# Blocks of up products as seven products of sums, in the second feed-forward network of a diffusion step

## The chip, the cores and the metric

The kernel runs on one core of one Trainium2 chip. The time is that of one execution on the device, in microseconds (us). TensorE (PE, with its weight loads as PEld) multiplies, VectorE (DVE) and ScalarE (ACT) do element-wise work, GpSimd (POOL) has next to none here, and SyncE (SP) issues the transfers from memory (DMA). Each engine takes its own instructions in order; between engines they wait on semaphores.

## The reference

One inference step of a two-layer backbone, for 128 context tokens and 512 latent tokens of 1024 features. Layer 0 mixes tokens by a state-space scan, layer 1 by differential attention; a gated convolutional feed-forward network follows in each layer. That network is what the change touches:

```python
def conv_ffn(h, up_w, conv_w, conv_b, down_w):
    u = dwconv(h @ up_w, conv_w, conv_b)
    a, v = jnp.split(u, 2, axis=-1)
    return (jax.nn.silu(a) * v) @ down_w
```

`up_w` is 1024 x 5632 (2 x 2816), `down_w` 2816 x 1024; `dwconv` is a convolution over tokens of width 3, for each channel apart. All is in 32-bit floating point.

## The kernel before, in words

Activations stand with features on the 128 partitions and all 640 tokens (512 latent, then 128 context) along the columns: `h` is 8 tiles of 128 x 640, one for each feature tile k. To keep the accuracy of 32 bits with products of lower precision, every operand is split into a high part (`hi`, a rounded copy made by ScalarE) and a low part (`lo`, the difference, made by VectorE), and each product of tiles is three: high with high, high with low, low with high.

Weights come in units of at most 128 x 1024. `weight_units` (L1214) lists them in the order of their use. `prefetch` (L119) issues the transfer of a unit into one of four `raw` buffers (`RAW`), on the queue of SP; `cast` (L128) makes `whi` (ScalarE, L95) and `wlo` (VectorE, L101), in one of five pairs of buffers (three with tag `w`, two with tag `x`). `nextw` (L147) hands out the next unit, prefetches three ahead and casts one ahead.

`ffn` (L601) works in three stages (`SUB`): up products for 9, 7 and 6 pairs of tiles, each stage followed by the down products of the part that is done. A pair p is one tile of the gate half a and one of the value half v of the hidden features. `dense_many` (L158) makes one up tile `up` of 128 x 640 in a PSUM buffer of two banks (1024 columns, three buffers with tag `d`): for each of 8 feature tiles three products, each in two column parts of 256 and 384 columns ("A", "B"), 48 products in all. The first three up tiles of a network are made ahead in `start_tiles` (L316; named `st`), while the normalisation still delivers `h` half by half; so pair 0 and half of pair 1 come from there.

After each tile `copy_out` (L607) copies it to `uraw` (ScalarE). `epilogue` (L613) then does for both halves the convolution (`conv`, L593: one ScalarE scaling, then four VectorE steps, of 511 and 127 columns twice), a Silu on ScalarE (`ca`), the gate product on VectorE (`cv`), and the split of the result into `mh` and `ml`, which the down products (`po`) take. `gate_add` (L278) adds the down tiles to the residual `xr` on VectorE.

The framework lays out each engine's instructions ahead of time, from the order in which the program emits them, their dependencies and priorities; what it has laid out is a fixed queue for each engine when the program runs. Dependencies are followed tile by tile: a write to one part of a PSUM tile waits for a reader of the other part.

Of the kernel before, what the change touches and what calls it, by code (L numbers as in the profile page):

```python
# [18 lines left out]
P = 128  # L19
D = 1024  # L20
KT = D // P
TP = 128
TS = 512
T = TP + TS
# [11 lines left out]
FT = FH // P  # L36
SUB = ((0, 8), (8, 15), (15, 22))
DA_SCALE = 64 ** -0.5
LAM_INIT = 0.8 - 0.6 * math.exp(-0.3 * 1)
RAW = 4  # L40
ATT_SPLIT = 6
NF = 19
RSQRT_MAGIC = float(0x5F3759DF)
# [2 lines left out]
class Step:  # L46
# [53 lines left out]
    def tt(self, out, a, b, op):  # L100
        return self.nc.vector.tensor_tensor(out, a, b, op)  # L101

    def mm(self, out, lhsT, rhs, start, stop):
        return self.nc.tensor.matmul(out, lhsT, rhs, start=start, stop=stop)  # L104

    def ct(self, shape, name, dt=F32):
        return self.pc.tile(shape, dt, tag=name, name=name)
# [11 lines left out]
    def prefetch(self, upto):  # L119
        while len(self.wraw) <= min(upto, len(self.units) - 1):  # L120
            u = len(self.wraw)
            ap, n = self.units[u]
            r = self.pw.tile([P, 1024], F32, tag="raw", name=f"raw{u}", bufs=RAW)
            dst = r[:, :n]
            self.nc.sync.dma_start(dst.rearrange("p (i c) -> p i c", i=ap.shape[1]) if len(ap.shape) == 3 else dst, ap)
            self.wraw[u] = r

    def cast(self, upto):  # L128
        while len(self.wcast) <= min(upto, len(self.units) - 1):
            u = len(self.wcast)  # L130
            self.prefetch(u)
            n = self.units[u][1]
            r = self.wraw[u]
            wp, t, b = (self.pw, "w", 3) if self.px is None or u % 5 < 3 else (self.px, "x", 2)
            hi = wp.tile([P, 1024], F32R, tag=t + "hi", name=f"whi{u}", bufs=b)
            lo = wp.tile([P, 1024], F32R, tag=t + "lo", name=f"wlo{u}", bufs=b) if u else None
            if u == 0:
                half = lambda t, j: t.rearrange("p (k j m) -> p k j m", k=KT, j=2)[:, :, j, :]
                r3 = r[:, :n].rearrange("p (k m) -> p k m", k=KT)
                self.act(half(hi, 0), r3, AF.Copy)  # L140
                self.tt(half(hi, 1), r3, half(hi, 0).bitcast(F32), ALU.subtract)
            else:
                self.act(hi[:, :n], r[:, :n], AF.Copy)
                self.tt(lo[:, :n], r[:, :n], hi[:, :n].bitcast(F32), ALU.subtract)
            self.wcast[u] = (hi, lo)

    def nextw(self):  # L147
# [411 lines left out]
    def mod_rest(self, l, t0, pool):  # L559
# [5 lines left out]
        for c in range(2):  # L565
            sb = self.pw.tile([P, 1024], F32, tag="raw", name="csil", bufs=RAW)
            self.act(sb, cb[:, c, :], AF.Tanh, scale=0.5)
# [33 lines left out]
    def ffn(self, l, h, nextnorm, pool):  # L601
        nc = self.nc
        cw = pool.tile([P, 2 * FT, 4], F32, tag="fcw", name=f"fcw{l}", bufs=1)
        nc.sync.dma_start(cw, self.a["fcw"][l])
        mid = {}

        def copy_out(ps):  # L607

            u = self.slot("f", "uraw", bufs=NF)
            self.act(u, ps[:, PO:PO + T], AF.Copy)  # L610
            return u

        def epilogue(p, ua, uv):  # L613
            ca = self.tmp("ca")
            self.conv(ca, ua, cw[:, p, :])
            cv = self.tmp("cv")
            self.conv(cv, uv, cw[:, FT + p, :])
            self.act(ca, ca, AF.Silu)
            self.tt(cv, ca, cv, ALU.mult)
            hi = self.slot("mh", f"mh{p}", F32R, bufs=9, pool=pool)  # L620
            lo = self.slot("ml", f"ml{p}", F32R, bufs=9, pool=pool)
            self.act(hi, cv, AF.Copy)
            self.tt(lo, cv, hi.bitcast(F32), ALU.subtract)
            mid[p] = (hi, lo)

        def pair(p):
            ua = copy_out(self.next_tile(h, "up"))
            epilogue(p, ua, copy_out(self.next_tile(h, "up")))

        self.start_tiles(h)  # L630
        done = 0
        for s, (k0, k1) in enumerate(SUB):
            self.down = False
            while done < min(k1 + 1, FT):
                pair(done)
                done += 1
            self.down = True
            if s == len(SUB) - 1 and self.modtask:
# [530 lines left out]
    def attention(self, h, nextnorm, pool):  # L1169
# [8 lines left out]
        for hd in range(8):  # L1178
# [35 lines left out]
    def weight_units(self):  # L1214
        a = self.a
        u = [(a["w_dt"], 512)]
        xbc = lambda g: [16 + 4 * g + t for t in range(4)] + [32 + g, 36 + g]
        z = lambda g: [4 * g + t for t in range(4)]
        order = xbc(0) + xbc(1) + z(0) + xbc(2) + z(1) + xbc(3) + z(2) + z(3)
        u += [(a["w_in"][j], 1024) for j in order]  # L1220
        for hf in range(2):
            u += [(a["w_so"][i, :, hf * 1024:(hf + 1) * 1024], 1024) for i in range(KT)]

        def ffn(l):
            done = 0
            out = []
            for k0, k1 in SUB:
                while done < min(k1 + 1, FT):
                    out.extend([(a["w_up"][l, done], 1024), (a["w_up"][l, FT + done], 1024)])
                    done += 1  # L1230
                out.extend([(a["w_dn"][l, i, :, k0 * P:k1 * P], (k1 - k0) * P) for i in range(KT)])
            return out

        u += ffn(0)
        for hd in range(8):
            u += [(a["w_qkv"][8 * j + hd], 1024) for j in range(3)]
        c = ATT_SPLIT * P
# [143 lines left out]
```

## Time and profile before

| | |
|---|---|
| median of 3 runs | 1879.16 us (1878.75 to 1879.62) |
| profiled execution | 1880.65 us |
| its span | 1878.9 us |
| TensorE busy | 1838.2 us, 98% of the span |
| VectorE busy | 1369.5 us, 73% |
| ScalarE busy | 952.9 us, 51% |
| chain that ended last | PE 91%, DVE 4%, ACT 3%, DMA 1% |

The page gives the busy time of each engine, the chain of work that ended last (followed back from the last instruction, each step to what released it), and groups of instructions by line, engine, operation and tiles: busy time and the mean duration of one in ns, then the idle time of the engine just before them and what ended it. Most operations go through helpers, so a line number says only which helper it was (L104 a product, L95 ScalarE, L98 and L101 VectorE), and the tile names tell what it was for. In lines in order of time, the first number is the start in us from the start of the span, the second the length; equal neighbours are merged (`x4`). Views of a stretch give busy time of PE, PEld, DVE, ACT and POOL, then the granted TensorE clock as a share of full speed.

### The profile page before, as it was taken

How to read it: one execution, taken by the hardware profiler on the slowest of the kernel's cores; microseconds unless marked ns; L12 is line 12 of the kernel's file. 1: busy time of each engine (PE TensorE's matmuls, PEld its weight loads, DVE VectorE, ACT ScalarE, POOL GpSimd, SP SyncE). 2: the span in 40 equal slices, each digit the busy share in tenths (PEclk: the TensorE clock that was granted, in tenths of full speed). 3: DMA queues.
4: the chain of work that ended last, by engine and by line, in shares of the span. 5: the costliest groups of instructions: out<-in, count | busy, mean ns of one | idle time of the engine just before them, and what ended most of it. 6: DMA issues, size and time to landing. Idle time of an engine off the chain costs nothing.

```text
span 1878.9 us, 32832 instructions
## 1 busy us (share of the span) xinstructions
PE 1838.2 (98%) x13322; PEld 1741.9 (93%) x13322; DVE 1369.5 (73%) x2637; ACT 952.9 (51%) x1745; POOL 0.2 (0%) x4
## 2 busy tenths in 40 slices
PE   7999999999999999999999999999999999999997
PEld 5899999999999999999999988888899999999996
DVE  5699999999658999974555877788777543553554
ACT  3489687878336441441443656566445432431441
POOL 0000000000000000000000000000000000000000
PEclk9999999999999999999999999999999999999998
DMA  9835243436624556532222212111122222122211
GB/s 337 266 121 147 97 147 109 140 115 202 199 80 142 185 180 221 181 103 91 68 68 78 79 40 65 58 50 48 61 88 89 69 79 80 63 72 89 64 40 57
DMA packets 79679, 209.74 MB, mean 112 GB/s; under 512 B 9276, under 2 KB 16040, under 8 KB 79400
## 3 DMA queue, kind: packets, MB, share of 16 engines
q1 hardware_dynamic: 78952, 207.13, 33.5%
q8 instruction: 104, 1.70, 0.4%
q10 hardware_dynamic: 576, 0.52, 0.1%
q14 instruction: 47, 0.39, 0.1%
HBM read 201.66 MB, written 5.96 MB: 111 GB/s over the span
## 4 chain that ended last, share of the span: by engine, by line
PE 91%; DVE 4%; ACT 3%; DMA 1%; issue 1%; SPq 0%; DVEq 0%; ACTq 0%
PE up L104 31%; PE po L104 25%; PE z L104 6%; PE x L104 5%; PE st L104 5%; PE bc L104 3%; PE yp L104 3%; PE q L104 2%; PE v L104 2%; PE k L104 1%; PE modrow L104 1%; PE sl L104 1%; PE in L104 1%; ACT whi L95 1%; ACT e L95 1%; PE ov L104 1%
## 5 line engine op out<-in xcount | busy, mean ns | idle before, releaser
L95 ACT ACTIVATE whi<-raw 128x1024 fp32r<-128x1024 f32 (+3 forms) x227 | 234.2, 1033 | 387.2 <-PE po L104 239.6
L101 DVE TENSOR_TENSOR wlo<-raw,whi 128x1024 fp32r<-128x1024 f32 (+2 forms) x226 | 269.2, 1192 | 172.2 <-ACT whi L95 165.1
L98 DVE SCALAR_TENSOR_TENSOR xr<-po,mod,xr 128x256 f32<-128x256 f32 (+2 forms) x231 | 89.2, 433 | 162.0 <-PE po L104 161.8
L104 PE MATMUL po<-mh,whi 128*128 128x256 f32 (+1 forms) x704 | 167.8, 310 | 0.0
L104 PE MATMUL po<-ml,whi 128*128 128x256 f32 (+1 forms) x704 | 167.5, 310 | 0.0
L104 PE MATMUL po<-mh,wlo 128*128 128x256 f32 (+1 forms) x704 | 167.3, 310 | 0.0
L104 PE MATMUL up<-h11h,wlo 128*128 128x256 f32 (+1 forms) x656 | 149.4, 309 | 0.0
L104 PE MATMUL up<-h01h,wlo 128*128 128x256 f32 (+1 forms) x656 | 149.4, 308 | 0.0
L104 PE MATMUL up<-h01h,whi 128*128 128x256 f32 (+1 forms) x656 | 149.3, 308 | 0.0
L104 PE MATMUL up<-h01l,whi 128*128 128x256 f32 (+1 forms) x656 | 149.3, 308 | 0.0
L104 PE MATMUL up<-h11l,whi 128*128 128x256 f32 (+1 forms) x656 | 149.3, 308 | 0.0
L104 PE MATMUL up<-h11h,whi 128*128 128x256 f32 (+1 forms) x656 | 149.3, 308 | 0.0
L104 PEld LDWEIGHTS po<-mh,whi 128*128 128x128 f32 x704 | 128.5, 188 | 0.7 <-ACT mh L95 0.5
L104 PEld LDWEIGHTS po<-mh,wlo 128*128 128x128 f32 x704 | 128.8, 188 | 0.0
L104 PEld LDWEIGHTS po<-ml,whi 128*128 128x128 f32 x704 | 128.6, 188 | 0.0
L104 PEld LDWEIGHTS up<-h01h,whi 128*128 128x128 f32 x656 | 119.3, 188 | 0.0
L104 PEld LDWEIGHTS up<-h01h,wlo 128*128 128x128 f32 x656 | 119.3, 188 | 0.0
L104 PEld LDWEIGHTS up<-h01l,whi 128*128 128x128 f32 x656 | 119.3, 188 | 0.0
L104 PEld LDWEIGHTS up<-h11h,whi 128*128 128x128 f32 x656 | 119.2, 188 | 0.0
L104 PEld LDWEIGHTS up<-h11h,wlo 128*128 128x128 f32 x656 | 119.2, 188 | 0.1
L104 PEld LDWEIGHTS up<-h11l,whi 128*128 128x128 f32 x656 | 119.2, 188 | 0.0
L98 DVE SCALAR_TENSOR_TENSOR ca<-uraw,fcw,ca 128x511 f32<-128x511 f32 (+1 forms) x176 | 85.2, 546 | 11.6 <-ACT ca L95 11.6
(497 smaller groups left out, 4315.6 us busy)
## 6 DMA issues: line engine op xcount, KB each, us to landing
raw<-in_w_up SPq DMA_DIRECT2D x88, 512.0 KB, 3.5
mw<-in_modT SPq DMA_DIRECT2D x48, 512.0 KB, 3.5
raw<-in_w_in SPq DMA_DIRECT2D x40, 512.0 KB, 5.5
rb<-rowd SPq DMA_DIRECT2D x40, 512.0 KB, 5.6
raw<-in_w_dn SPq DMA_DIRECT2D x32, 448.0 KB, 3.2
raw<-in_w_qkv SPq DMA_DIRECT2D x24, 512.0 KB, 3.5
mr<-in_mod SPq DMA_DIRECT2D x44, 256.0 KB, 5.7
mp<-in_modp SPq DMA_DIRECT2D x32, 256.0 KB, 5.4
```

What stands on the lines that cost most here:

```text
L95: return self.nc.scalar.activation(out, in_, func, **k)
L98: return self.nc.vector.scalar_tensor_tensor(out, in0, s, in1, op0, op1)
L101: return self.nc.vector.tensor_tensor(out, a, b, op)
L104: return self.nc.tensor.matmul(out, lhsT, rhs, start=start, stop=stop)
```

## The change

From pair 2 on (`S0`), in the second network alone, a pair of up tiles is computed together by `pair7`. Its four first feature tiles (k = 0 to 3) are taken as a product of 2 x 2 blocks: the weights have two blocks of two feature tiles in each half (a and v), the activations have two blocks of feature tiles and two blocks of 320 tokens (`TH`). Such a product needs eight products of blocks; here it is made of seven (`block`, each 2 feature tiles x 3 terms), on sums and differences of blocks, with some results used in more than one of the four output blocks. Feature tiles 4 to 7 (`rest`) are multiplied as before, but in column halves of 320.

On the side of the activations the sums (`t12`, `t43`) and their high and low parts (`Th`, `Tl`, `T3`) are made once, by `operands`, when pair 2 begins. On the side of the weights they are made for each pair by a unit without a transfer (`ap is None`), which stands in the list between the unit of a and that of v: four VectorE sums of 256 columns, then two casts of 512 on ScalarE and two on VectorE. The v unit's cast leaves out its first 256 columns. On the output side one accumulator is copied out while it grows (`ua` left, then `ua` right with `p5` added, then `uv`), and others are added from PSUM on VectorE. `epilogue` is as before. `prefetch` runs six units ahead in `pair7`.

```diff
@@ cast
+            elif sums:
+                self.prefetch(u + 1)
+                ra, rv = self.wraw[u - 1], self.wraw[u + 1]
+                w = NS * P
+                s12, s34 = (self.slot("f", nm, bufs=NF) for nm in ("s12", "s34"))
+                self.tt(s12[:, :w], rv[:, :w], rv[:, w:2 * w], ALU.add)
+                self.tt(s12[:, w:2 * w], s12[:, :w], ra[:, :w], ALU.subtract)
+                self.tt(s34[:, :w], ra[:, :w], rv[:, :w], ALU.subtract)
+                self.tt(s34[:, w:2 * w], ra[:, w:2 * w], s12[:, w:2 * w], ALU.subtract)
+                for j, s in enumerate((s12, s34)):
+                    c = slice(2 * w * j, 2 * w * (j + 1))
+                    self.act(hi[:, c], s[:, :2 * w], AF.Copy)
+                    self.tt(lo[:, c], s[:, :2 * w], hi[:, c].bitcast(F32), ALU.subtract)
             else:
-                self.act(hi[:, :n], r[:, :n], AF.Copy)
-                self.tt(lo[:, :n], r[:, :n], hi[:, :n].bitcast(F32), ALU.subtract)
+                c = slice(c0 // 2, n)
+                self.act(hi[:, c], r[:, c], AF.Copy)
+                self.tt(lo[:, c], r[:, c], hi[:, c].bitcast(F32), ALU.subtract)
...
@@ ffn
+        def block(ps, w, c0, xs, first, last, more=False):
+            hi, lo = w
+            for i, (xh, xl) in enumerate(xs):
+                c = slice(c0 + i * P, c0 + (i + 1) * P)
+                self.mm(ps, hi[:, c], xh, first and i == 0, False, more)
+                self.mm(ps, hi[:, c], xl, False, False, more)
+                self.mm(ps, lo[:, c], xh, False, last and i == len(xs) - 1, more)
+                if i % 2:
+                    self.hook()
+
+        def operands():
+            cut = lambda t, j: t[:, j * TH:(j + 1) * TH]
...
+            for i in range(NS):
+                f1, f2 = self.tmp("f1"), self.tmp("f2")
+                for f, k in ((f1, i), (f2, NS + i)):
+                    self.tt(f, h[k][0].bitcast(F32), h[k][1].bitcast(F32), ALU.add)
+                t12, t43 = self.slot("f", "t12", bufs=NF), self.slot("f", "t43", bufs=NF)
+                self.tt(cut(t12, 0), cut(f1, 1), cut(f1, 0), ALU.subtract)
+                self.tt(cut(t12, 1), cut(f2, 1), cut(t12, 0), ALU.subtract)
+                self.tt(cut(t43, 0), cut(f2, 0), cut(t12, 1), ALU.subtract)
+                self.tt(cut(t43, 1), cut(f2, 1), cut(f1, 1), ALU.subtract)
...
+                for o, x in ((slice(0, T), t12), (slice(T, T + TH), cut(t43, 0))):
+                    self.act(hi[:, o], x, AF.Copy)
+                    self.tt(lo[:, o], x, hi[:, o].bitcast(F32), ALU.subtract)
+                self.act(cut(t3, 0), cut(t43, 1), AF.Copy)
+                self.tt(cut(t3, 1), cut(t43, 1), cut(t3, 0).bitcast(F32), ALU.subtract)
...
+        def pair7(p, B, Ts, rest):
...
+            self.prefetch(u + 6)
+            self.cast(u + 2)
...
+            ps = self.dense_ps("up")
+            X, Y = ps[:, :TH], ps[:, 512:512 + TH]
+            block(X, wa, 0, B11, True, True)
+            with self.tc.high_priority():
+                self.act(ua[:, lft], X, AF.Copy)
+            block(Y, wa, w, B21, True, False)
+            ps = self.dense_ps("up")
+            V, Z = ps[:, :TH], ps[:, 512:512 + TH]
+            block(V, ws, 0, T1, True, True)
+            with self.tc.high_priority():
+                self.act(p5, V, AF.Copy)
+            block(X, ws, w, T2, False, True, True)
+            with self.tc.high_priority():
+                self.tt(ua[:, rgt], X, p5, ALU.add)
+            block(Y, wa, r0, rest[0], False, True)
+            self.tt(ua[:, lft], Y, ua[:, lft], ALU.add)
+            block(Z, ws, 3 * w, B22, True, False)
+            self.cast(u + 3)
+            block(Z, wa, r0, rest[1], False, True)
+            self.tt(ua[:, rgt], Z, ua[:, rgt], ALU.add)
+            block(X, ws, 2 * w, T3, False, True, True)
+            with self.tc.high_priority():
+                self.act(uv[:, rgt], X, AF.Copy)
+            self.cast(u + 4)
+            block(V, wv, r0, rest[1], False, True, True)
+            self.tt(uv[:, rgt], V, uv[:, rgt], ALU.add)
+            block(X, wv, w, T4, False, True, True)
+            block(X, wv, r0, rest[0], False, True, True)
+            self.act(uv[:, lft], X, AF.Copy)
+            epilogue(p, ua, uv)
+
         def pair(p):
+            if l and p >= S0:
+                if p == S0:
+                    self.sevens = operands()
+                return pair7(p, *self.sevens)
...
@@ weight_units
-                    out.extend([(a["w_up"][l, done], 1024), (a["w_up"][l, FT + done], 1024)])
+                    sums = [(None, 1024)] if l and done >= S0 else []
+                    out.extend([(a["w_up"][l, done], 1024), *sums, (a["w_up"][l, FT + done], 1024)])
```

More of the change, by code (lines that the diff above doesn't have):

```diff
@@ L40 @@
 RAW = 4
+NS = 2
+S0 = 2
+TH = T // 2
 ATT_SPLIT = 6
@@ L101, in tt, with mm @@
         return self.nc.vector.tensor_tensor(out, a, b, op)
-    def mm(self, out, lhsT, rhs, start, stop):
-        return self.nc.tensor.matmul(out, lhsT, rhs, start=start, stop=stop)
+    def mm(self, out, lhsT, rhs, start, stop, more=False):
+        return self.nc.tensor.matmul(out, lhsT, rhs, start=start, stop=stop, skip_group_check=more)
     def ct(self, shape, name, dt=F32):
@@ L122, in prefetch @@
             ap, n = self.units[u]
+            if ap is None:
+                self.wraw[u] = None
+                continue
             r = self.pw.tile([P, 1024], F32, tag="raw", name=f"raw{u}", bufs=RAW)
@@ L133, in cast @@
             r = self.wraw[u]
+            sums = self.units[u][0] is None
+            c0 = 2 * NS * P if u and self.units[u - 1][0] is None else 0
             wp, t, b = (self.pw, "w", 3) if self.px is None or u % 5 < 3 else (self.px, "x", 2)
@@ L624, in epilogue @@
             mid[p] = (hi, lo)
+        def block(ps, w, c0, xs, first, last, more=False):
[9 more added lines that the diff above has]
+            cut = lambda t, j: t[:, j * TH:(j + 1) * TH]
+            B = [[[tuple(cut(t, j) for t in h[NS * k + i]) for i in range(NS)] for j in range(2)] for k in range(2)]
+            Ts = [[], [], [], []]
+            for i in range(NS):
[7 more added lines that the diff above has]
+                self.tt(cut(t43, 1), cut(f2, 1), cut(f1, 1), ALU.subtract)
+                hi, lo = (pool.tile([P, 3 * TH], F32R, tag=f"T{nm}{i}", name=f"T{nm}{i}", bufs=1) for nm in "hl")
+                t3 = self.slot("f", f"T3_{i}", F32R, bufs=NF)
+                for o, x in ((slice(0, T), t12), (slice(T, T + TH), cut(t43, 0))):
[3 more added lines that the diff above has]
+                self.tt(cut(t3, 1), cut(t43, 1), cut(t3, 0).bitcast(F32), ALU.subtract)
+                Ts[0].append((cut(hi, 0), cut(lo, 0)))
+                Ts[1].append((cut(hi, 1), cut(lo, 1)))
+                Ts[2].append((cut(t3, 0), cut(t3, 1)))
+                Ts[3].append((cut(hi, 2), cut(lo, 2)))
+            rest = [[tuple(cut(t, j) for t in h[k]) for k in range(2 * NS, KT)] for j in range(2)]
+            return B, Ts, rest
@@ new lines, in pair7 @@
+        def pair7(p, B, Ts, rest):
+            (B11, _), (B21, B22) = B
+            T1, T2, T3, T4 = Ts
+            u = self.wi
+            self.wi += 3
+            self.prefetch(u + 6)
+            self.cast(u + 2)
+            wa, ws, wv = (self.wcast[u + j] for j in range(3))
+            w, r0 = NS * P, 2 * NS * P
+            ua, uv = (self.slot("f", "uraw", bufs=NF) for _ in range(2))
+            p5 = self.slot("f", "p5", bufs=NF)[:, :TH]
+            lft, rgt = slice(0, TH), slice(TH, T)
+            ps = self.dense_ps("up")
[28 more added lines that the diff above has]
+            epilogue(p, ua, uv)
```

## The prediction

> **What bounds the kernel now.** I read the page's busy shares first, then the chain of work that ended last, then busy time by stretch, then the groups by shape inside the second feed-forward network, and last the order of time on VectorE and ScalarE where the change begins.
>
> ```profile
> PE 1838.2 (98%) x13322; PEld 1741.9 (93%) x13322; DVE 1369.5 (73%) x2637; ACT 952.9 (51%) x1745; POOL 0.2 (0%) x4
> ...
> 1416.16 105.73 PE up L104 x720
> 1521.90 56.00 PE po L104 x384
> 1577.90 98.64 PE up L104 x672
> ...
> 1726.47 84.53 PE up L104 x576
> ...
> 1430.00:1521.00 91.00, 91.00 (x623) 91.00 (x622) 52.08 (x79) 43.73 (x53) 0.00 (x0) 1.00 0.25 82
> ```
>
> The first line is the page's engine table, the next four are steps of the chain (start, length, what), the last is busy time in one stretch (sum, then PE, PEld, DVE, ACT, POOL, granted clock, DMA share, GB/s). In the second network TensorE works without a gap: the three runs of up products last 105.73, 98.64 and 84.53 us, and in 91 us of the first TensorE is busy for 91, VectorE for 52, ScalarE for 44. The full clock is granted. So TensorE products alone set the time there, and fewer of them would shorten it, as long as the other two engines keep up.
>
> ```profile
> L104 PE MATMUL up<-h11l,whi 128*128 128x384 f32 x328 | 110.8, 338 | 0.0
> L104 PE MATMUL up<-h11h,wlo 128*128 128x256 f32 x328 | 91.6, 279 | 0.0
> ...
> L98 DVE SCALAR_TENSOR_TENSOR ca<-uraw,fcw,ca 128x511 f32<-128x511 f32 x44 | 32.9, 748 | 7.7 <-ACT ca L95 7.7
> L98 DVE SCALAR_TENSOR_TENSOR xr<-po,mod,xr 128x256 f32<-128x256 f32 x42 | 18.4, 480 | 75.8 <-PE po L104 75.8
> L101 DVE TENSOR_TENSOR cv<-ca,cv 128x640 f32<-128x640 f32 x22 | 18.1, 825 | 0.7
> L98 DVE SCALAR_TENSOR_TENSOR ca<-uraw,fcw,ca 128x127 f32<-128x127 f32 x44 | 15.2, 345 | 0.0
> L98 DVE SCALAR_TENSOR_TENSOR h11l<-nt,mod,h11h 128x256 fp32r<-128x256 f32 x8 | 3.8, 481 | 0.0
> L101 DVE TENSOR_TENSOR nsq<-nsq,sqt 128x256 f32<-128x256 f32 x4 | 1.7, 416 | 0.0
> ...
> L95 ACT ACTIVATE uraw<-up 128x640 f32<-128x640 f32 x41 | 28.2, 687 | 0.0
> L95 ACT ACTIVATE mh<-cv 128x640 fp32r<-128x640 f32 x22 | 16.2, 738 | 57.3 <-DVE cv L101 57.3
> L95 ACT ACTIVATE sqt<-xr 128x384 f32<-128x384 f32 x4 | 2.1, 527 | 0.9 <-DVE xr L98 0.9
> ```
>
> These are groups by shape from 1400 us on (busy, mean ns of one, idle before). A duration is not a price: products overlap. 105.73 / 720 gives 0.1468 us from one product to the next, at a mean of 320 columns; the records of a 384 and a 256 together last 617 ns but take 294, so a result stands about 0.2 us behind the end of its columns (estimate). For VectorE and ScalarE the price comes from the starts of neighbours in order of time:
>
> ```profile
> 1420.95 1.22 DVE L101 TENSOR_TENSOR wlo<-raw,whi 128x1024 fp32r<-128x1024 f32 x1
> 1422.09 0.82 DVE L101 TENSOR_TENSOR cv<-ca,cv 128x640 f32<-128x640 f32 x1
> 1422.82 1.67 DVE L98 SCALAR_TENSOR_TENSOR ca<-uraw,fcw,ca 128x511 f32<-128x511 f32 x3
> ...
> 1425.14 0.34 DVE L98 SCALAR_TENSOR_TENSOR ca<-uraw,fcw,ca 128x127 f32<-128x127 f32 x1
> 1425.41 1.22 DVE L101 TENSOR_TENSOR wlo<-raw,whi 128x1024 fp32r<-128x1024 f32 x1
> 1426.54 1.93 DVE L98 SCALAR_TENSOR_TENSOR cv<-uraw,fcw,cv 128x511 f32<-128x511 f32 x4
> 1428.39 1.22 DVE L101 TENSOR_TENSOR wlo<-raw,whi 128x1024 fp32r<-128x1024 f32 x1
> ...
> 1443.34 0.82 DVE L101 TENSOR_TENSOR ml<-cv,mh 128x640 fp32r<-128x640 f32 x1 [0.81 <-ACT mh L95]
> ...
> 1423.92 0.68 ACT L95 ACTIVATE uraw<-up 128x640 f32<-128x640 f32 x1
> 1424.50 1.05 ACT L95 ACTIVATE whi<-raw 128x1024 fp32r<-128x1024 f32 x1
> 1425.46 0.91 ACT L95 ACTIVATE cv<-uraw,fcw 128x640 f32<-128x640 f32 x1
> 1426.27 0.72 ACT L95 ACTIVATE ca<-ca 128x640 f32<-128x640 f32 x1
> ```
>
> Start to start a tensor-tensor operation of 1024 columns holds VectorE for 1.13 us (1425.41 to 1426.54), one of 640 for 0.73 (1422.09 to 1422.82), the four convolution steps for 1.85, the step of 127 for 0.27. A straight line through 640 and 1024 gives estimates of 0.39 for 320, 0.32 for 256, 0.59 for 512 and 0.87 for 768 columns. ScalarE: 0.58 for a copy of 640, 0.96 for 1024, 0.81 for a scaled 640.
>
> **Part 1: products saved.** A pair of up tiles is 96 products before (2 tiles, 8 feature tiles, 3 terms, 2 column parts) and 90 after: seven blocks of 6, and four of 12 for the feature tiles left as they are. All 90 have 320 columns, the mean of before, and load weights as often as before, once each. 20 pairs (2 to 21) take part: 120 x 0.1468 = 17.6 us, a pair 13.21 instead of 14.09. This is the ceiling, and all of it is on the path.
>
> **Part 2: the operands, once.** The sums of feature blocks are emitted at pair 2, and VectorE takes its queue in order. The third product of pair 2's third block waits for the low part of the first half of the weight sums; in the changed program's order this stands behind everything that follows. Up to the step at 1425.14 the queue is that of before, less 0.27 for a cast of 768 columns in place of 1024 at 1420.95, so this step starts at 1424.87. From it on: that step 0.27; four f of 640 columns, 2.92; one convolution 1.85; the gate product and ml of pair 1, 1.46; eight differences of 320, 3.12; Tl, two of 640 and two of 320, 2.24; the low parts of T3, two of 320, 0.78; a cast of 1024 for pair 3, 1.13; four weight sums of 256, 1.28. Together 15.05, to 1439.9. ScalarE's high part of 512 columns (about 0.63, between 527 and 738 ns) starts when the third weight sum is done, 0.3 earlier, and VectorE's low part needs about 0.69 more (between 416 and 825 ns): TensorE goes on at 1441.0. ScalarE is done with each of its shares before VectorE wants it, so its queue adds nothing else.
>
> TensorE would want that product at 1416.16 + 48 x 0.1468 (the fourth tile) + 14 x 0.1468 = 1425.2. It stands for about 15.8 us. What is queued behind on TensorE is all of pair 2, and nothing else is there to fill in: after the first block the second waits too, for a ScalarE copy that stands behind the T copies, so that the gap is some 14 us in one piece. Bounds: 14.5 us if each of the 30 operations holds the queue 0.04 less; 18.5 if each costs its full duration, 0.09 more (825 against 730 ns).
>
> **Part 3: the clock after it.**
>
> ```profile
> 1082.20:1085.60 3.40, 1.15 (x12) 0.88 (x12) 3.02 (x5) 1.71 (x6) 0.00 (x0) 1.00 0.27 77
> 1085.60:1089.00 3.40, 3.22 (x12) 3.22 (x13) 1.21 (x3) 2.21 (x6) 0.00 (x0) 0.50 0.22 82
> ```
>
> In attention TensorE was busy for 1.15 of 3.4 us, and in the next 3.4 us half the clock was granted, with 12 products done. At half clock 3.4 us of work take 1.7 us too long. A gap of 14 us earns at least that. I take 1.7, with 0 and 3.4 (two such stretches) as ends. [...]
>
> **Part 4: what a pair costs after that.** VectorE per pair before: 3.70 for two convolutions, 1.46, two casts 2.26: 7.4 of 14.1. After: 3.70, 1.46, casts of 1024, 768 and twice 512 (3.18), four sums of 256 (1.28), four adds of 320 out of PSUM (1.56): 11.2 of 13.2. In order, it also waits twice on ScalarE, 0.8 for the high part of the weight sums (after the last ua add ScalarE scales 0.81, copies about 0.35, casts 1024 in 0.96 and 512 in 0.63, to 3.3 with the first hand-over, when VectorE has three sums and one convolution step behind it, 2.5) and 0.81 for mh, as in the row of 1443.34: about 13.1. It fits, by 0.1 to 0.4 us. No row has a 320-column add out of PSUM. The xr row (PSUM, 480 ns) and the h11l row (SBUF, 481) at 256 columns say that PSUM costs nothing more, so 0.39; ends 0.32 (256 columns) and 0.73 (640). [...]
>
> ScalarE: copies of 320 four times (about 0.3 each), 3.0 for casts, 1.6 for convolutions, 1.3 for silu and mh: 7.1 of 13.2. Room enough, but one of its copies is on the path. The accumulator of the first block is copied to ua before TensorE may write the next block into the same tile. In the steady order ScalarE has, from the end E of the pair before: the last uv copy (from E + 0.2, about 0.45 long, between the halved 687 ns and 527), the convolution scaling (from E + 0.65, holds 0.81), and only then the ua copy, from E + 1.46 to E + 1.9. TensorE has 11 products in between, 1.61. It waits 0.3 us in each pair. Ends: 0 if ScalarE takes the copy first, 0.8 if the copies last as long as those of 640. The other exchanges have room: the p5 add 13 products, the T3 copy 12, the ua adds 6 (0.88 against about 0.7, the tightest).
>
> So a pair takes 13.5, with 13.2 and 14.8 as ends; 14.8 is VectorE at full durations with no overlap: 2.99 + 1.38 + 1.65 + 3.56 (casts) + 1.66 + 1.92, and the two waits of 0.8. I take 13.5, nearest to the starts of neighbours, which is how back-to-back work of this queue ran. Sixteen pairs save 0.57 each, and pairs 2, 3, 9 and 16, where VectorE has no pair behind it or has caught up, up to 0.88: 9.1 + 3.0 to 3.5, taken as 12, or 11 with the tight ua adds slipping now and then.
>
> ```profile
> raw<-in_w_up SPq DMA_DIRECT2D x88, 512.0 KB, 3.5
> ```
>
> **At no cost.** The row is the page's group of up weight loads (count, size, us from issue to landing). The weight sums move no byte: the queue of loads has the same entries in the same order, two of 512 KB a pair, and each raw buffer is given back one pair ahead; without that lead 3.5 us of a load would show. At the two returns from the down products the weight sums of the next pair are cast before the last down tile, with VectorE idle there; without this each return would pay 1.28 + 0.63 + 0.69 us, less the 1.76 of two blocks. The final epilogue has the length of before.
>
> **The sum.** + 15.8 + 1.7 - 11 = + 6.5 us. The profiled execution took 1880.65 us (span 1878.9, 1.75 around it), the median of the runs is 1879.16, 0.08% below; the difference carries over: about 1886 us.
>
> **Rivals.**
> 1. The per-pair wait is hidden (ScalarE's copy comes in time, and the ua adds too). For it: ScalarE is half idle; against: its order is fixed, with the convolution first. Saving 17.6: 1879.16 + 17.5 - 17.6 = 1879, no change.
> 2. VectorE becomes the bound. For it: 13.1 of 13.2, with no row for its new shapes. From 14.1 a pair nothing is saved: 1879.16 + 17.5, 1896; at the end of 14.8, 1911.
> 3. Faster: TensorE's stop at pair 2 is short. It decides from 13.8 us all told with the full saving (17.6 - 13.8 = 3.8, 0.2%); at 10 us it would be 1872. For it: the feature tiles are ready before the first up tile starts, so the work has no data to wait for. Against: it needs VectorE to run 15 us of queued work in 10, and the queue keeps its order.
> 4. The count does not turn into time, because 320 columns run slower than the mean of 256 and 384. Before has no full-height row of it; both ends are linear, so I give this little: at 0.160 a product a pair is 14.4, and the time 1879 + 17.5 + 6, 1903.
>
> **Chances.** A measurement of this kernel tells about 0.2% (3.8 us) from no change: below 1875.4 is faster, above 1882.9 slower. Forecast (13.4 to 13.8 a pair, 1882 to 1892): 0.58. Rival 1: 0.17. Rival 2: 0.16. Rival 3: 0.06. Rival 4: 0.03. Rival 1 lies within 0.2% but for 0.01 below it, and 0.03 of the forecast lies within too. So faster 0.07, same 0.19, slower 0.74. The range goes from rival 1 to the near side of rival 2, 1879 to 1895 (left out are rivals 3 and 4 and some 0.1 of rival 2); the likeliest case alone has 1882 to 1892.
>
> **What would show it.** A TensorE gap of about 14 us after the first block of pair 2, with VectorE busy on f, t, Tl and s throughout, and half the clock once behind it; up products 120 fewer at 0.147 us each; then a short TensorE wait on the ScalarE uraw copy in nearly every pair; pairs 13.5 us apart. It is wrong if the gap is under 10 us, if pairs are over 13.9 apart with TensorE waiting for VectorE's adds, or if the products themselves take longer.

## The result and the profile after

The changed kernel takes 1885.07 us (median of 10 runs, 1881.10 to 1888.89), the kernel before, run beside it, 1878.89 us (10 runs, 1877.45 to 1881.52). The ratio is 1.0032, with a 95% interval of 1.0023 to 1.0042: slower by about 6 us. The profiled execution took 1887.62 us with a span of 1885.8, against 1880.65 and 1878.9 before: 6.9 us more in the span.

First the engine table of the changed kernel's page, its largest group of up products, and what TensorE waited for from 1400 us on (us in total, times, longest):

```profile
PE 1829.6 (97%) x13202; PEld 1727.3 (92%) x13202; DVE 1455.7 (77%) x2855; ACT 973.0 (52%) x1831; POOL 0.2 (0%) x4
...
L107 PE MATMUL up<-h11h,whi 128*128 128x320 f32 (+1 forms) x456 | 141.2, 316 | 14.9 <-ACT uraw L98 14.6
...
PE up L107 <- ACT uraw L98: 14.6, 6, 13.7
PE nbc L107 <- DVE rs_y L101: 2.5, 1, 2.5
PE ms L107 <- ACT sq L98: 0.7, 1, 0.7
PE up L107 <- ACT whi L98: 0.4, 1, 0.4
```

There are 120 products fewer, and TensorE is busy for 8.6 us less than the 1838.2 of before. In their place stands 14.6 us of waiting for ScalarE's copies of up products, 13.7 of it in one piece. That piece in the order of time, on TensorE and then on VectorE (start, length, what, and in brackets the idle time before it and its releaser):

```profile
1437.12 0.64 PE L107 MATMUL up<-h11h,whi 128*128 128x320 f32 x1 [13.65 <-ACT uraw L98]
1439.50 0.64 PE L107 MATMUL up<-Th,whi 128*128 128x320 f32 x1 [0.41 <-ACT whi L98]
1440.23 0.64 PE L107 MATMUL up<-Th,wlo 128*128 128x320 f32 x1
```

```profile
1423.73 0.35 DVE L101 SCALAR_TENSOR_TENSOR ca<-uraw,fcw,ca 128x127 f32<-128x127 f32 x1
...
1428.44 0.50 DVE L104 TENSOR_TENSOR t<-f,f 128x320 f32<-128x320 f32 x1
1428.85 0.50 DVE L104 TENSOR_TENSOR t<-f,t 128x320 f32<-128x320 f32 x1
...
1439.48 1.29 DVE L104 TENSOR_TENSOR wlo<-s,whi 128x512 fp32r<-128x512 f32 x2 [0.24 <-ACT whi L98]
```

Pair 2 began at 1422.42 us. Its third product of the third block (Th with wlo) would follow 14 products later, at 1424.48; it stood at 1440.23, 15.75 us late. From the step at 1423.73 to the low part of the weight sums at 1439.48 VectorE worked with no pause longer than the 0.24 us that the last line shows. An operation of 320 columns holds its queue for 0.41 us here (1428.44 to 1428.85).

The granted clock around it, by stretches (sum, then PE, PEld, DVE, ACT, POOL busy, clock, DMA share, GB/s):

```profile
1424.20:1438.00 13.80, 0.88 (x3) 0.88 (x4) 13.80 (x26) 4.90 (x10) 0.00 (x0) 0.65 0.00 1
1438.00:1442.00 4.00, 3.59 (x14) 2.96 (x13) 2.50 (x6) 1.45 (x3) 0.00 (x0) 0.50 0.62 200
1442.00:1446.00 4.00, 4.00 (x19) 4.00 (x19) 0.49 (x1) 0.14 (x1) 0.00 (x0) 0.59 0.16 67
```

Half the clock (0.50) was granted from 1428.2 to 1445.3. Products stood 0.267 us apart in it instead of 0.147: from 1440.23 on, 18 of them took 4.97 us instead of 2.64, 2.3 us more. So pair 2 lost 15.75 + 2.3 = 18.1 us.

Behind pair 2, the chain of work that ended last, over one pair (start, length, what; left out are steps of VectorE and ScalarE between 1489.33 and 1495.25):

```profile
1481.13 0.45 ACT uraw L98
...
1481.60 0.93 ACT cv L98
1482.53 0.33 ACT uraw L98
...
1482.90 6.43 PE up L107 x42
...
1495.25 0.92 ACT cv L98
1496.17 0.33 ACT uraw L98
...
1496.54 11.84 PE up L107 x79
```

In nine of the nineteen pairs behind pair 2 the chain passes through these three steps of ScalarE: the copy of the last uv block, the convolution's scaling (cv), the copy of the next pair's first block; then TensorE goes on, at 1482.90 and again 13.64 us later. At 1482.39 it takes 0.51 us to the next product instead of 0.147, and 0.25 to the one after: 0.46 us lost. Ten of the nineteen pairs take 0.35 to 0.51 us at this place, the other nine 0.17 to 0.26. From the T3 block of one pair to that of the next it is 13.50 to 13.66 us inside the three stages, 0.3 to 0.45 above 90 x 0.1468, 13.21, and 13.06 to 13.38 to the last pair of a stage. What was saved is the 18.1 less the 6.9 by which the span grew: 11.2 us. Counted at the products it is a little more: between the starts of products the nineteen pairs lose about 5.9 us, and 17.6 less 5.9 is 11.7; where the other 0.5 us of the span lie is not shown.

### The profile page after: what moved, and what is told of

It reads as the page before. It is cut to its first block, busy times and chain, and to the rows that moved or that the text cites. A ratio compares the mean times of both kernels' runs of the same rounds, so it can differ in the third digit from the quotient of the medians.

```text
span 1885.8 us, 32904 instructions
## 1 busy us (share of the span) xinstructions
PE 1829.6 (97%) x13202; PEld 1727.3 (92%) x13202; DVE 1455.7 (77%) x2855; ACT 973.0 (52%) x1831; POOL 0.2 (0%) x4
## 4 chain that ended last, share of the span: by engine, by line
PE 86%; DVE 7%; ACT 4%; issue 1%; DMA 1%; SPq 0%; DVEq 0%; ACTq 0%
PE up L107 28%; PE po L107 25%; PE z L107 6%; PE x L107 5%; PE st L107 4%; PE bc L107 3%; PE yp L107 3%; PE q L107 2%; ACT whi L98 1%; PE k L107 1%; PE modrow L107 1%; PE sl L107 1%; PE in L107 1%; ACT e L98 1%; PE ov L107 1%
## 5 line engine op out<-in xcount | busy, mean ns | idle before, releaser
L98 ACT ACTIVATE whi<-raw 128x1024 fp32r<-128x1024 f32 (+3 forms) x227 | 229.4, 1012 | 326.9 <-PE po L107 205.2
L104 DVE TENSOR_TENSOR wlo<-raw,whi 128x1024 fp32r<-128x1024 f32 (+2 forms) x226 | 264.0, 1169 | 77.4 <-ACT whi L98 72.2
L107 PE MATMUL up<-h11h,whi 128*128 128x320 f32 (+1 forms) x456 | 141.2, 316 | 14.9 <-ACT uraw L98 14.6
L107 PE MATMUL up<-h11l,whi 128*128 128x320 f32 (+1 forms) x456 | 139.9, 310 | 0.0
L107 PE MATMUL up<-h11h,wlo 128*128 128x320 f32 (+1 forms) x456 | 137.0, 310 | 0.0
L107 PEld LDWEIGHTS up<-h11h,whi 128*128 128x128 f32 x456 | 85.8, 189 | 20.0 <-ACT uraw L98 19.1
L98 ACT ACTIVATE mh<-cv 128x640 fp32r<-128x640 f32 x44 | 32.5, 738 | 121.2 <-DVE cv L104 121.2
L101 DVE SCALAR_TENSOR_TENSOR ca<-uraw,fcw,ca 128x511 f32<-128x511 f32 (+1 forms) x176 | 89.0, 548 | 4.7 <-ACT ca L98 4.7
L101 DVE SCALAR_TENSOR_TENSOR cv<-uraw,fcw,cv 128x511 f32<-128x511 f32 (+1 forms) x176 | 85.8, 547 | 5.8 <-ACT cv L98 5.8
```

The lines of the kernel that those rows point to most:

```text
L98: return self.nc.scalar.activation(out, in_, func, **k)
L101: return self.nc.vector.scalar_tensor_tensor(out, in0, s, in1, op0, op1)
```

## The experiments

The theory was that of the prediction: the change wins on TensorE, loses 18 us at one place because the sums of feature blocks stand in VectorE's queue right before their use, and leaves a third of the rest in a wait on one ScalarE copy. The rivals were that the added work of VectorE and ScalarE costs something everywhere, and that products of 320 columns are slower. All times are medians beside runs of the kernel before (1878.74 to 1879.73); each ratio is to that kernel.

| Kernel | us | ratio, 95% interval |
|---|---|---|
| changed kernel | 1885.07 | 1.0032 [1.0023, 1.0042] |
| start at pair 9 | 1871.38 | 0.9960 [0.9948, 0.9973] |
| second half of the epilogue later | 1885.94 | 1.0036 [1.0023, 1.0048] |
| gap filled with products | 1882.88 | 1.0018 [1.0009, 1.0027] |
| products alone | 1865.43 | 0.9932 [0.9918, 0.9945] |
| Y in its own bank | 1878.05 | 0.9993 [0.9984, 1.0002] |
| operands at the start | 1878.88 | 0.9996 [0.9987, 1.0005] |
| operands at the start, from pair 4 | 1881.33 | 1.0008 [1.0000, 1.0017] |
| operands at the start, Y bank | 1869.95 | 0.9951 [0.9937, 0.9965] |
| start at pair 9, Y bank | 1867.78 | 0.9939 [0.9927, 0.9952] |
| operands split, from pair 5, Y bank | 1864.99 | 0.9922 [0.9910, 0.9935] |
| operands split, from pair 6, Y bank | 1865.03 | 0.9924 [0.9910, 0.9938] |

### The stop: start behind the first down products

```diff
-S0 = 2
+S0 = 9
```

> The change starts at pair 9 instead of pair 2, which is the first pair behind the first run of down products. The differences and sums of feature blocks are then emitted under the down products, where TensorE has other work. 13 pairs take part. Theory (the stop at pair 2 is what makes the change lose): no TensorE gap over 1 us at pair 9 and no half clock there; 13 pairs save 0.5 to 0.6 us each as in the changed kernel, 7 to 8 us in all, and the time is 1871 to 1872 us. Rival A (the stop only moves with the operands, because the down stage needs VectorE too): a gap of some 10 us or later down products, 1885 us or more. Rival B (what VectorE and ScalarE do more in each pair costs everywhere, and the stop is not the main term): 1879 us or more with no gap.

Measured: 1871.38 us, 7.5 below the kernel before (by its ratio). The chain through this place (start, length, what), and the first and the last of the sums of feature blocks on VectorE:

```profile
1500.00 22.49 PE up L107 x153
1522.49 56.00 PE po L107 x384
1578.49 21.57 PE up L107 x143
...
1524.47 0.82 DVE L104 TENSOR_TENSOR f<-h11h,h11l 128x640 f32<-128x640 f32 x1
...
1541.46 0.48 DVE L104 TENSOR_TENSOR T<-t,T 128x320 fp32r<-128x320 f32 x1
```

The same operations now lie between 1524 and 1542, under 56.00 us of down products, which take as long as before; TensorE goes from one stage to the other without a stop, and the clock stays whole (1.00 from 1500 to 1580). Pairs stay at 13.50 to 13.66, but for a few (13.39 to 13.90): 13 of them save about 0.55 each against 14.09, 7.2 us. With the stop gone the change is faster, so the stop is the larger term; rivals A and B fall.

### The clock: the gap filled

```diff
+            if p == S0:
+                pf = self.bank("m", "fill")
+                for _ in range(88):
+                    self.mm(pf[:, :TH], wa[0][:, :P], B11[0][0], True, True)
             block(Y, wa, w, B21, True, False)
```

> 88 products of 320 columns that nobody reads are added behind the first block of pair 2, so that TensorE has 88 x 0.1468 = 12.9 us of work in its gap of 13.65 us; all else is the changed kernel. Theory (half the clock behind the gap costs some 2.3 us, the wait for VectorE the rest): the clock stays whole, the third product of the third block still starts near 1440.2 us, the products behind it stand 0.147 us apart, and the time is 1882.5 to 1883.5 us. Rival A (the half clock costs nothing that shows): 1885 us as in the changed kernel. Rival B (it is the larger part of the loss at pair 2): below 1880 us.

Measured: 1882.88 us, as expected, but not wholly for the reason given. By stretches:

```profile
1424.00:1435.80 11.80, 11.80 (x83) 11.80 (x82) 11.80 (x22) 4.13 (x8) 0.00 (x0) 1.00 0.00 1
1435.80:1439.00 3.20, 1.53 (x9) 1.00 (x7) 3.17 (x8) 1.17 (x3) 0.00 (x0) 1.00 0.00 0
1439.00:1442.40 3.40, 3.09 (x11) 3.09 (x12) 1.34 (x3) 1.06 (x3) 0.00 (x0) 0.50 0.80 299
1442.40:1446.40 4.00, 4.00 (x27) 3.82 (x27) 0.98 (x2) 0.16 (x1) 0.00 (x0) 1.00 0.03 12
```

Under the filling products the clock stayed whole, but the fill ended early: in the next 3.2 us TensorE was busy for 1.53, and the 3.4 us behind that ran at half, which cost 11 products 0.12 us each, 1.3 us. From its first product to its T3 block pair 2 took 25.07 us instead of 26.04, so the trace shows 1.0 us won, the shortening of the half clock. The medians differ by 2.2, with intervals that just overlap. The stop itself stayed (the block of Th began at 1439.31), so VectorE's queue is the larger part of the loss and rival B falls; rival A falls with the 1.0 us.

### The wait in each pair: two edits

The first edit moved the second half of the epilogue behind the next pair's third exchange:

```diff
             self.conv(ca, ua, cw[:, p, :])
+            if l and p >= S0:
+                self.late_cv = (p, ca, uv)
+            else:
+                finish(p, ca, uv)
+
+        def finish(p, ca, uv):
             cv = self.tmp("cv")
...
                 self.act(p5, V, AF.Copy)
+            if self.late_cv:
+                finish(*self.late_cv)
+                self.late_cv = None
```

> From pair 2 on the second half of a pair's epilogue (the convolution of its second tile, silu, the gate product and its split) is emitted behind the third exchange of the next pair, so that ScalarE takes the copy of the first block ahead of the convolution's scaling. The stop at pair 2 stays. Theory (the wait of TensorE in each pair is this one ScalarE copy behind that scaling): the wait on the copy goes, pairs stand 13.2 to 13.3 us apart instead of 13.6, 20 x 0.35 is about 6 us, and the time is 1878 to 1880 us. Rival (a pair is held by the sum of VectorE's work, or by the products of 320 columns): pairs stay at 13.5 to 13.6 us with the wait at another exchange, 1884 to 1886 us.

Measured: 1885.94 us, no gain. ScalarE in this kernel, in order of time:

```profile
1481.05 0.44 ACT L99 ACTIVATE uraw<-up 128x320 f32<-128x320 f32 x1 [0.92 <-PE up L108]
1481.52 0.92 ACT L99 ACTIVATE cv<-uraw,fcw 128x640 f32<-128x640 f32 x1
1482.34 0.42 ACT L99 ACTIVATE uraw<-up 128x320 f32<-128x320 f32 x1
```

The scaling still stands ahead of the copy. The lines moved, but the order on ScalarE did not; probably the framework's plan had the scaling ready before the copy, which no run shows. So this run tells nothing of the wait; only of the edit.

The second removes the reason for the wait. The accumulators X and Y are halves of one tile, and the second block, into Y, waits for the copy of X:

```diff
-            X, Y = ps[:, :TH], ps[:, 512:512 + TH]
+            X, Y = ps[:, :TH], self.bank("m", "y")[:, :TH]
```

> The accumulator Y gets a bank of its own instead of the second half of the tile that holds X, so that the second block of a pair need not wait until ScalarE has copied the first block out of X; the copy is wanted six products later, before the block that adds to X. All else, the stop at pair 2 too, is the changed kernel. Theory (0.3 us a pair is lost to this one copy behind the convolution's scaling, and VectorE keeps up): the short wait goes, pairs stand 13.2 to 13.4 us apart, 20 x 0.25 is 5 us, and the time is 1879 to 1881 us. Rival A (VectorE or another exchange takes the wait over): pairs stay at 13.5 to 13.6 us, 1884 to 1886 us. Rival B (a bank of its own costs a wait elsewhere): above 1887 us.

Measured: 1878.05 us, 7 below the changed kernel. Its chain over the same pairs, the busy time in three of them (columns as above), and TensorE's longest wait, at pair 2:

```profile
1479.93 1.76 PE up L107 x12
1481.69 1.75 PE y L107 x12
1483.45 8.80 PE up L107 x60
1492.25 0.88 PE y L107 x6
1493.13 1.76 PE up L107 x12
1494.88 1.75 PE y L107 x12
1496.64 8.80 PE up L107 x60
...
1480.00:1521.00 41.00, 41.00 (x282) 41.00 (x281) 36.87 (x68) 24.60 (x39) 0.00 (x0) 1.00 0.30 91
...
1440.38 0.64 PE L107 MATMUL y<-h11h,whi 128*128 128x320 f32 x1 [13.13 <-DVE uraw L104]
```

ScalarE has left the chain, and pairs stand 13.19 us apart (1483.45 to 1496.64): 90 products of 0.1466. VectorE is busy for 36.87 of 41 us, 11.9 of each 13.19, and holds nothing up. The stop at pair 2 is still there, but shorter, which the expectation had not allowed for. With Y in its own bank TensorE's order changed too: 24 products of pair 2, and not 6, now stand ahead of the gap, the gap is 13.13 us (it ends with a VectorE add that stands behind the sums in VectorE's queue), the 72 products from 1441.01 on take 11.81 us (1.25 more than at 0.1466 each), and between the starts of products pair 2 loses 14.9 us instead of 18.1. So the traces put 3.2 us of the gain on pair 2 and 6.1 on the waits of the other pairs, 0.3 each; together they are the 9.3 us between the two profiled spans (1885.8 and 1876.5), of which the medians show 7. What the bank does to a pair is therefore read from the 13.19, and not from the 7 us.

### The products alone

The sums and their casts are left out: blocks of the feature tiles stand for the sums of feature blocks, and the pair's own weights for the sums of weights. The output is then not that of the network.

```diff
-            self.wi += 3
-            self.prefetch(u + 6)
-            self.cast(u + 2)
-            wa, ws, wv = (self.wcast[u + j] for j in range(3))
+            self.wi += 2
+            self.prefetch(u + 4)
+            self.cast(u + 1)
+            wa, wv = (self.wcast[u + j] for j in range(2))
+            ws = wa
...
-                    self.sevens = operands()
+                    self.sevens = (B, (B[0][0], B[0][1], B[1][0], B[1][1]), rest)
```

> The products of the change alone: blocks of the feature tiles stand in the place of the sums of feature blocks, and the weights of the pair in the place of the sums of weights, so that these sums and their casts are left out and the result is another; 120 products fewer, the exchanges and their order stay. Theory (a product of 320 columns takes 0.147 us, and what is lost in a pair is the copy behind the convolution's scaling, not the load of VectorE): no stop, pairs still 13.4 to 13.6 us apart with the short wait on ScalarE's copy, 20 x 0.55 is 11 us saved, 1866 to 1869 us. Rival A (the wait comes from the added casts and sums): pairs 13.2 us apart, 17.6 us saved, 1861 to 1862 us. Rival B (VectorE's other work, or products that take longer, holds the pair): pairs of 13.6 us or more with no wait on that copy, 1870 us or more.

Measured: 1865.43 us, 13 below the kernel before. Pairs stand 13.36 us apart, between the theory and rival A. ScalarE at the place of the wait:

```profile
1476.70 0.75 ACT L98 ACTIVATE uraw<-up 128x320 f32<-128x320 f32 x2
1477.34 0.92 ACT L98 ACTIVATE cv<-uraw,fcw 128x640 f32<-128x640 f32 x1
```

Here the planner put both copies (x2) ahead of the scaling, so the expectation of the same wait was wrong. What is left is 0.17 us a pair: 0.06 at the first product behind the exchange (0.21 instead of 0.147) and 0.10 at the next (0.25). It speaks for the order on ScalarE as the cause, with the bank run, and against slow products of 320 columns; by itself it can't tell the order from the work left out, since both changed.

### Where the sums can go

The next six kernels ask whether the stop is only a matter of place. The first three have the sums at the start of the network; the diff is that of the first.

```diff
         self.start_tiles(h)
+        if l:
+            self.sevens = operands()
...
-                if p == S0:
-                    self.sevens = operands()
```

> The sums and differences of feature blocks are emitted right behind the start of the first two up tiles instead of at pair 2; VectorE then has them ahead of pair 0's convolutions, under 42 us of products of pairs 0 and 1. All else is the changed kernel. Theory (the stop is only the place of the operands in VectorE's queue, not their amount): no gap and no half clock at pair 2, 15.8 + 2.3 us less than the changed kernel, 1866 to 1869 us. Rival A (VectorE is late all the same, since the same 12 us of work now delay the weights' low parts and the epilogues of pairs 0 and 1): a gap of some us in pairs 0 to 2, 1872 to 1880 us. Rival B (the stop moves whole to the start of the network): 1883 us or more.

> As before, with the sums of feature blocks emitted right behind the start of the first up tiles, but the change starts at pair 4, so that four plain pairs, 56 us of products, lie over them; 18 pairs take part. Theory (no stop in either, the two more pairs are worth what a pair saves): two pairs x 0.55 us slower than with the start at pair 2, 1867 to 1870 us. Rival (pairs 2 and 3 of the earlier start still pay for the operands): 1 us or more faster than with the start at pair 2.

> Both edits: the sums of feature blocks right behind the start of the first up tiles, and Y in a bank of its own. Theory (the two losses are independent): both gains add up, no gap, pairs 13.2 to 13.4 us apart, 1861 to 1864 us, 15 to 18 us below the kernel before. Rival (VectorE then becomes the bound, with 11.2 us of work and its waits in 13.2): pairs of 13.5 us, 1866 to 1869 us.

Measured: 1878.88, 1881.33 and 1869.95 us. All three lie 6 to 11 us above what was expected. For the first, in order of time, TensorE's gap, the last low part of the feature tiles on VectorE, and ScalarE:

```profile
1421.73 0.90 PE L107 MATMUL up<-h11h,whi 128*128 128x256 f32 x2 [6.89 <-ACT uraw L98]
```

```profile
1411.29 0.35 DVE L101 SCALAR_TENSOR_TENSOR h11l<-nt,mod,h11h 128x128 fp32r<-128x128 f32 x1
...
1416.64 0.45 ACT L98 ACTIVATE T<-t 128x320 fp32r<-128x320 f32 x1
1419.99 0.74 ACT L98 ACTIVATE Th<-t 128x640 fp32r<-128x640 f32 x1 [2.89 <-DVE t L104]
...
1420.99 0.69 ACT L98 ACTIVATE uraw<-st 128x640 f32<-128x640 f32 x1
```

The feature tiles are ready only at 1411.6, when the first up tiles, begun before it, are three microseconds from their end. ScalarE's copy that frees those tiles stands behind its copies of T, one of which waits 2.89 us for VectorE's t. TensorE needs the freed tile at 1414.8 and gets it at 1421.7, and the clock is halved until 1426.0 (0.50 from 1421.7 on). So the stop did not vanish; a shorter one (6.9 us in place of 13.65, and waits of 0.9, 0.2 and 0.3 us at pair 2) stands at the start. With the start at pair 4 the gap is 7.4 us, with 1.2 and 0.3 at pair 4; with the Y bank 4.25 and, at pair 2, 1.4. Rival A of the first of these had the time and the kind: the same work delays other work, here ScalarE's copies. The two more plain pairs of the second gain nothing, since the longest gap lies before them; with the bank pairs are 13.19 apart (13.22 and 13.37 at first), so VectorE is no bound there either.

Behind the normalised tiles and in two portions, one per plain pair, with the Y bank:

```diff
-S0 = 2
+S0 = 5
...
-        def operands():
+        def operands(i):
...
-                if p == S0:
-                    self.sevens = operands()
                 return pair7(p, *self.sevens)
+            if l and p in (2, 3):
+                self.sevens = operands(p - 2)
```

> Y in a bank of its own, the change from pair 5 on (17 pairs), and the sums of feature blocks in two halves, one emitted with the plain pair 2, one with the plain pair 3, so that VectorE has two plain pairs and most of a third between them and their use. Theory (the stop is work of 12 us that TensorE's plain products can cover if it stands far enough ahead of its use and behind the normalised feature tiles): no TensorE gap over 2 us from pair 0 on, no half clock, pairs 13.2 us apart against 14.1, 17 x 0.9 is 15.3 us saved, 1863 to 1865 us. Rival (VectorE is still behind from the first pairs, and is late at pair 5): a gap of 2 to 6 us there, 1866 to 1871 us.

> The same one pair later: the change from pair 6 on (16 pairs), the halves of the sums with the plain pairs 3 and 4. Theory: no stop in either kernel, so one pair x 0.9 us slower than with the start at pair 5, 1864 to 1866 us. Rival (the start at pair 5 still pays for late operands): faster than with the start at pair 5.

> Y in a bank of its own, and the change from pair 9 on, behind the first run of down products, with the sums of feature blocks in one piece there (13 pairs). Theory (the two losses are independent, and the operands cost nothing under the down products): 13 x 0.9 is 11.7 us below the kernel before, 1866 to 1868 us, 4 us below the same start without the bank. Rival (the wait in each pair was hiding VectorE's load): 1870 to 1872 us, as without the bank.

Measured: 1864.99, 1865.03 and 1867.78 us. The start at pair 5, what TensorE waited for from 1380 us on, and the stretch that holds the stop in the changed kernel; behind it the same stretch of the changed kernel:

```profile
PE nbc L107 <- DVE rs_y L101: 2.5, 1, 2.5
PE ms L107 <- ACT sq L98: 1.6, 2, 0.9
PE st L107 <- ACT h11h L98: 0.3, 1, 0.3
...
1405.00:1516.00 111.00, 111.00 (x744) 110.04 (x744) 93.44 (x173) 64.96 (x98) 0.00 (x0) 1.00 0.25 76
```

```profile
1405.00:1516.00 111.00, 96.35 (x612) 94.28 (x611) 92.13 (x180) 59.40 (x96) 0.00 (x0) 0.92 0.19 62
```

No wait for up products is left, the clock is whole, and TensorE does 744 products in 111 us where the changed kernel does 612. Pairs stand 13.19 apart, but for one of 13.37. This is faster than both kernels, by 0.8% against the one before. Sixteen and seventeen pairs cannot be told apart by these medians (0.04 us, where one pair is worth 0.9); both save 13.7 us where 14.4 and 15.3 were expected. The start at pair 9 with the bank saves 11.0 of the expected 11.7, and 3.6 more than without it.

## Why the prediction was right

The time came out 0.9 us below the 1886 forecast, and the terms on TensorE's path were there, in kind and about in size. That the sum is so near is in part luck: the clock was taken 0.6 us too low and what is saved up to 0.7 too low, which cancel, and the runs of the changed kernel spread over 8 us.

- **Products.** 120 fewer at 0.1468: confirmed. Without the wait a pair takes 13.19 us, 90 x 0.1466. Rival 4, slower products, is out.
- **The stop.** Forecast 15.8 us, measured 15.75. VectorE's queue took 15.5 us to the end of the last weight sum (1439.25) where 15.05 was counted, and began 1.3 us after pair 2's first product instead of 1.7; these errors cancel. The price read from the starts of neighbours held: 0.41 for 320 columns (0.39 estimated). The gap after the first block was 13.65 (14 forecast), ended by a copy behind the T copies, as said.
- **The clock.** Forecast 1.7 us, measured 2.3, within its ends of 0 and 3.4. This term was undersized: one stretch of 3.4 us at half was counted, but the clock came back 5.1 us after the product at 1440.23 began. Each us at half also costs less than was taken, since products stood 1.82 times as far apart (0.267 us against 0.147) and not twice.
- **The wait in each pair.** Forecast 0.3 us on ScalarE's copy behind the convolution's scaling; measured 0.3 on average, but 0.1 to 0.5 in single pairs. The bank run shows it as the cause: with the wait for that copy taken away, pairs stand at 13.19. In each wait some 0.10 us of this lies between the first product behind the wait and the next (0.25 us instead of 0.147, as at 1482.90), which no row of before showed. Pairs 9 and 16, taken as free of waits, lost about 0.4 each, while six others, taken at 0.3, lost about 0.2 or less.
- **What is saved.** Forecast 11 us, measured 11.2 by the span and 11.7 by the products. The step from 12 to 11, for ua adds that slip, was worked out from no row; the trace shows one short wait on an add of this kind (0.18 us from product to product instead of 0.147, at 1530.72) and one on the p5 add in each of pairs 9 and 16 (0.23). The sum of +6.5 came out as 6.9 in the span and 6.2 in the medians.
- **At no cost.** TensorE's waits have one entry for weights, 0.4 us at pair 2 itself, so sums of weights and loads held nothing else up. The two returns from the down products are those of pairs 9 and 16, with their 0.4 us.
- **VectorE fits.** Forecast 13.1 of 13.2 with its waits; the terms named there (11.2, 0.8 and 0.81) add up to 12.8, and no run shows the other 0.3. The changed kernel could not show this, since its pairs were longer; the bank run does, at 11.9 us busy of 13.19. The add of 320 columns out of PSUM, for which no row stood, holds the queue for 0.40 us (1493.23 to 1493.63), as the differences out of SBUF do (0.41). Rival 2 is out.
- **Rivals 1 and 3.** Rival 1's 1879 is near the 1878.05 of the bank run, where the wait is hidden; but there pair 2 also lost 3.2 us less, so the nearness is in part luck. Rival 3 was given the argument that the feature tiles are ready before the first up tile starts. That is wrong: with the sums moved ahead their last low part is written at 1411.3, when the first up tiles are nearly done.

What stays open: what the rest of the 2.2 us between the filled and the changed kernel is, if it is no noise (the trace shows 1.0 for the clock), why the place of the wait takes 0.21, 0.36 or 0.51 us in different pairs, and why the bank run's median gained 7 us where its profile gained 9.3.

## What to carry to other kernels

Fewer products were worth their time here only where the operands were made far enough ahead of use (1885.07 us with the sums right before it, 1864.99 with the sums in two halves under plain pairs and Y in its own bank). Price the queue of the engine that makes them from its last item before the need (15.5 us here), not from the engine's share of busy time (77%), and place them under work that does not need them, once their inputs are ready. Two accumulators in one tile were one dependency: the copy of one held up the other, and a bank of its own took pairs from 13.50 to 13.66 us to 13.19, while the edit of the order gained nothing (1885.94 us). Such an edit is only an edit if the engine's queue shows it.

## What the runs showed of the hardware that was not expected

- The stretches at half the clock (0.50) lasted 3.4 us in the filled kernel (1439.0 to 1442.4), 6.8 with the operands at the start (1419.2 to 1426.0; the start is worked out from the mean of 0.82 over the 6.9 us before 1421.7) and 17.1 in the changed kernel (1428.2 to 1445.3): about one, two and five times 3.4.
- The clock came back late. In the changed kernel TensorE worked from 1437.12 on with one pause of 0.41 us that the trace shows, and half the clock lasted until 1445.3. In the filled kernel a stretch of 3.2 us with 1.53 us of work was followed by 3.4 us at half.
- At half clock products of 320 columns stood 0.267 us apart in the changed kernel, 1.82 times the 0.147 at full clock and not twice.
- At full clock a product of 320 columns that followed a wait was followed by the next 0.25 us later (1482.90 to 1483.15 in the changed kernel, 1436.93 to 1437.18 in the filled one) and not 0.147, so such a wait cost some 0.10 us more than its length.
- VectorE at 90% busy (36.87 of 41 us in the bank run), with its low parts and adds on the way to TensorE, cost TensorE nothing there (41.00 of 41 us busy).
